# A hybrid retention and attention layer on one core: the first retention head's queries and keys move behind the attention branch's projection, four more gates become attention fillers whose results are put aside in device memory, and inputs and first weights alternate in one queue

## The chip, the cores and the metric

The kernel runs on one core of one Trainium2 chip. The metric is device time in microseconds, the median over runs of the whole program. The kernel before took 1144.44 us (three runs: 1139.92, 1144.44 and 1145.31). Of one execution there is a profile, taken by the hardware profiler. In the text, PE is TensorE's matrix multiplication and PEld its loading of weights, DVE is VectorE, ACT is ScalarE, POOL is GpSimd and SP is SyncE.

## The reference, cut to what matters

One layer over 512 tokens with a model width of 1024. Two branches read the same normalised input through one combined projection; each is projected back, gated, and their sum goes through an output projection. An MLP and a gated embedding follow.

```python
h = rms_norm(x, norm_mix)
rq, rk, rv, rg, cq, ckv, krope, gr, gm = jnp.split(h @ w_in, offsets, axis=-1)

rq = rope(rq, pos); rk = rope(rk, pos) * 256 ** -0.5      # 4 heads, 256 wide
ro = retention(rq, rk, rv)                                # chunks of 128 tokens, decay
a_ret = (rms_norm(ro, ret_norm) * silu(rg)) @ w_br        # w_br: 2048 x 1024

q = (rms_norm(cq, q_lat_norm) @ w_uq); kv = rms_norm(ckv, kv_lat_norm) @ w_ukv
mo = causal_block_attention(...)                          # 8 heads
a_mla = mo @ w_bm

mixed = sigmoid(gr) * a_ret + sigmoid(gm) * a_mla
x = x + mixed @ w_o
x = x + square(relu(rms_norm(x, norm_mlp) @ w_up)) @ w_down
x = x + sigmoid(rms_norm(x, norm_ple) @ w_ple_gate) * (p_l @ w_ple)
```

## The kernel before, in words

Activations lie with channels on the 128 partitions and the 512 tokens along the row, so a vector of 1024 channels is eight tiles of 128x512. Every product is made of three matmuls (`mm3`): an operand is split into a high and a low part, and low x high, high x low and high x high are accumulated in a PSUM bank. A projection of one tile of outputs from eight tiles of inputs is therefore 24 matmuls of 128x512. The high part of a tile is an ACT copy, the low part a DVE subtraction that follows it (`split`, L308 and L309 in the profile; for weights `load_chunk`, L265 and L267).

**The program order.** The kernel is a list of steps, written out by hand. A step may have a weight chunk. `run_steps` loads the chunk of the step after the current one (AHEAD = 1) before it emits the current step, so an engine's queue holds, in this order, the split of the next weights and then the work of this step. Each engine runs its queue strictly in order. Where nothing binds an instruction to its place (`keep_in_program_order`), the program's builder may put it ahead of steps before it, so the queues as built are shown with the change. Weight halves lie in NW = 3 rotating buffers each for high and low parts, the raw weights in NRAW = 6; taking a buffer waits for its former user. The raw weights come in by DMAs on SP's queue.

**Chunks that are sums.** The projections rv and rg (retention's values and gates) and the down projection are made by a seven-product scheme on 2x2 blocks. Its operands are sums and differences of blocks: of weights, by one DMA and a second one that accumulates on top of it, which POOL issues (`("sw", …)`, prepared PREP = 3 ahead); of activations, by `x_operand(p)`, p = 1 to 7, from the normalised input tiles `xr` (f32) and `xn` (their split, made by `norm_x`).

**Stages on PE**, in order of time: the first projection `a1` (tile pA), for which the input tiles `x` are multiplied by a gain and split (`xg`, L311) while the sum of squares is still to come; latents; eight attention heads, where softmax leaves gaps that **fillers** use; `branch_m` (tile bm, the attention branch's projection); then for two pairs of heads rv, and for each of the four heads rq, rk, rg, scores, and the former head's `branch_r` (tile br); then the gates gr and the last `branch_r`; out_proj (tile wo); the MLP (up, dn) and the gated embedding.

**Fillers** are half projections (12 matmuls each) from `xg`, the input that isn't yet divided by its root mean square; the result is multiplied by `rbc` (that factor, broadcast). Before there are 26 of them: the gates gm of the attention branch (8 x 2 halves, each result put in device memory by `aside`, a DMA that POOL issues), rq and rk of retention head 0 (4 x 2 halves), and the gate gr0 (2 halves). EARLY = 1 is the number of gr gates among the fillers.

**Tiles.** A pool T has 45 rotating tiles of 128x512 (NDYN), a pool K 16 (NKEEP). xg, and later xn, x_operands and much else lie in them.

**The tail before the output projection.** `reload(n)` brings back ret (the sum of the first three heads' branch_r, tile re) and the gated attention branch (tile ze), 16 loads on SP's queue. Then come the gates gr1 and gr2, and four steps of `branch_r(3)`, each of which makes two tiles of 24 matmuls together, with the gates gr3 to gr7 and `mix` between them. `ret_factor(3)` splits the last head's output (tiles og to rog) after gr1. `mix(n)` multiplies ret by the gate, adds the attention branch and splits the result (tile mix), which out_proj reads.

**The start.** ACT's queue issues the eight loads of x and the gains before its first arithmetic; SP's queue issues the weights wr_a. A DMA is issued only when the eighth DMA before it, of all queues, has landed.

Of the kernel before, what the change touches and what calls it, by code (L numbers as in the profile page):

```python
# [37 lines left out]
P = 128  # L38
S = 512
# [14 lines left out]

NDYN, NKEEP, NW, NRAW, NDRAW, AHEAD, PREP, EARLY, PAD = 45, 16, 3, 6, 4, 1, 3, 1, 104
GROUPS = DFF // 1024
# [14 lines left out]
def chunk_specs():  # L71
# [32 lines left out]
    for h in range(RH):  # L104
        for key, o in (("rq", O_RQ), ("rk", O_RK)):
            for n in range(2):
                if h:
                    add((key, h, n), "w_in", full, _rng(o + h * RQK + n * P, P))
                else:
                    for k in range(2):  # L110
                        add((key, h, n, k), "w_in", _rng(k * S, S), _rng(o + h * RQK + n * P, P))
        for k in range(4):
            add(("br", h, k), "w_br", _rng(h * RV, RV), _rng(2 * k * P, 2 * P))
# [38 lines left out]
def trunk_layer(ctx: ExitStack, tc: tile.TileContext, xT, pT, pos, gains, const, decay, wstream, outT):  # L152
# [207 lines left out]
    for k in range(8):  # L360
        xs.append(T(f"x{k}"))
        tc.keep_in_program_order(nc.scalar.dma_start(xs[k], xT[:, k]))
        if k == 0:
            tc.keep_in_program_order(nc.scalar.dma_start(gn, gains))
        if k < 6:
            prepare(("a1", k))
    tc.keep_in_program_order(nc.sync.dma_start(cst, const))
    tc.keep_in_program_order(nc.sync.dma_start(posi, pos.partition_broadcast(P)))
# [333 lines left out]
    def x_operand(p):  # L702
# [9 lines left out]
        for c in range(2):  # L712
            t = T(f"sy{c}") if p == 5 else V["sx"][c]
            for kk in range(2):
# [7 lines left out]
                else:  # L722
                    TT(o, xr[4 + k][:, lo_], o, op=ALU.subtract)

            new = T if p == 7 else K
            hl = split(t, None, hi=new(f"s{p}{c}h", F32R), lo=new(f"s{p}{c}l", F32R))
            XS[p].extend(cut(hl, kk * 256, 256) for kk in range(2))
# [36 lines left out]

    def ret_qk(w, h, key, n, half=None):
        d = R[h]
        if half is None:
            ps = proj(B(f"{key}{h}{n}"), xn, w)
        else:
            if half == 0:  # L770
                d["half"] = B(f"{key}{h}{n}")
            ps = proj(d["half"], xg, w, k0=4 * half, k1=4 * half + 4)
            if half == 0:
                return
        a, b = T(f"{key}a{h}{n}"), T(f"{key}b{h}{n}")
        TT(a, ps, V["cr"] if n == 0 else V["sr"], op=ALU.mult)
        TT(b, ps, V["sr"] if n == 0 else V["cr"], op=ALU.mult)
        if n == 0:
            d[key] = (a, b)
        else:  # L780
            a0, b0 = d[key]
            TT(a0, a0, a, op=ALU.subtract)
            TT(b0, b0, b, op=ALU.add)
            if half is not None:
                TT(a0, a0, V["rbc"], op=ALU.mult)
                TT(b0, b0, V["rbc"], op=ALU.mult)
            d[key] = (split(a0, f"{key}x{h}"), split(b0, f"{key}y{h}"))
# [64 lines left out]
    def ret_factor(h):  # L852
        d, r = R[h], R[h]["r"]
        bc = bcast(B(f"pbo{h}"), lambda b: r[:, b:b + 1])
        for m in range(4):
            TT(d["og"][m], d["og"][m], bc, op=ALU.mult)
            new = K if m < 2 else T
            d["rog"][m] = split(d["og"][m], None, hi=new(f"rog{h}{m}h", F32R), lo=new(f"rog{h}{m}l", F32R))

# [14 lines left out]
    def reload(n):  # L874
        for l, nm in ((ret, "re"), (zm, "ze")):
            t = T(f"{nm}{n}")
            nc.sync.dma_start(t, l[n])
            l[n] = t

    def gate_r(w, n, half=None):  # L880
        if half is None:
            ps = proj(B(f"gr{n}"), xn, w)
        else:
# [3 lines left out]
            if half == 0:  # L887
                return
        sgr[n] = T(f"gr{n}")
        if half is None:  # L890
            ACT(sgr[n], ps, AF.Sigmoid)
        else:
            TT(sgr[n], ps, V["rbc"], op=ALU.mult)

# [193 lines left out]
    fillers = [(("gm", n, half), gate_m, n, half) for n in range(8) for half in range(2)]  # L1088
    fillers += [((key, 0, n, half), ret_qk, 0, key, n, half) for key in ("rq", "rk") for n in range(2) for half in range(2)]

    fillers += [(("gr", n, half), gate_r, n, half) for n in range(EARLY) for half in range(2)]
# [37 lines left out]
    for h in range(MH):  # L1129
        p, more = h // 2, h + 2 < MH  # L1130
        step(None, scores, h)
        if h % 2 == 0:
# [12 lines left out]
            if h == 0:  # L1145
                fill(1)
            step(None, transposes, h)
            if h == 2:
                step(None, rotary_out, 1)
            if h:  # L1150
                fill(1)
        else:
# [25 lines left out]
    for n in range(8):  # L1178
        step(("bm", n), branch_m, n)
        if n < 2:  # L1180
            step(None, norm_x, 2 + n)
        elif n == 2:
            step(None, x_operand, 7)
        elif n < 7:
            step(None, norm_x, n + 1)
    for p in (1, 2, 6, 5, 4, 3):
        step(None, x_operand, p)
    for h in range(RH):
        for key in ("rq", "rk"):
            for n in range(2 if h else 0):  # L1190
                step((key, h, n), ret_qk, h, key, n)
                if (key, n) == ("rq", 0):
                    step(None, ret_factor, h - 1)
# [19 lines left out]
    for n in range(8):  # L1213
        step(None, reload, n)
    for n in range(EARLY, EARLY + 2):
        step(("gr", n), gate_r, n)
        if n == EARLY:
            step(None, ret_factor, RH - 1)
    for k in range(4):
        step(("br", RH - 1, k), branch_r, RH - 1, k)  # L1220
        step(None, mix, 2 * k)
        for n in (EARLY + 2 * k + 2, EARLY + 2 * k + 3):
            if n < 8:
                step(("gr", n), gate_r, n)
        step(None, mix, 2 * k + 1)
# [107 lines left out]
```

## Time and profile before

| | us |
|---|---|
| median of three runs | 1144.44 |
| the profiled execution | 1137.74 |
| its span (first to last instruction) | 1136.0 |
| outside the span | 1.74 |

| engine | busy us | share |
|---|---|---|
| PE | 1103.0 | 97% |
| DVE | 736.8 | 65% |
| ACT | 535.7 | 47% |
| POOL | 83.0 | 7% |

The granted clock of TensorE had a mean of 0.998 over the span. Stages on PE: first projection from 11.4 us, attention with its fillers from 56 to 242, branch_m from 242 to 285.7, retention to 636, gates and the last branch_r to 698, output projection to 742, MLP to 1084.

How to read it: busy times of the engines overlap, so they do not add up to the span. A matmul that is shown with 0.39 us starts 0.227 us after the one before it, since matmuls are pipelined, and a window counts those that only reach into it. "idle before" is the time in which an engine's queue stood, and the name behind it is the instruction for which it stood.

### The profile page before, as it was taken

The numbers are of one execution on the slowest core, as the hardware profiler recorded it, in microseconds if no ns is written. First come the engines' busy times: TensorE is split into PE (matmuls) and PEld (weight loads), VectorE is DVE, ScalarE is ACT, GpSimd is POOL, SyncE is SP. The second block draws the span as 40 slices with busy tenths as digits, with TensorE's granted clock in tenths as the row PEclk, the third lists the DMA queues.
The fourth block names the chain that finished last, engine by engine and source line by source line (L and its number), as shares of the span: only waits on it lengthen the run. The fifth ranks groups of instructions, "written<-read, shape, count | busy, mean of one in ns | idle before, by whom it ended". The sixth has DMA issues, their size and how long they took to land.

```text
span 1136.0 us, 14670 instructions
## 1 busy us (share of the span) xinstructions
PE 1103.0 (97%) x5540; PEld 935.0 (82%) x5540; DVE 736.8 (65%) x1205; ACT 535.7 (47%) x762; POOL 83.0 (7%) x108
## 2 busy tenths in 40 slices
PE   5999989999799999999999999999999999999998
PEld 4887878888589899889989888888888888888877
DVE  5787686766667746636764756546566566668775
ACT  5555656454456345445544423434444443445542
POOL 0000000001210110121011000010100100101000
PEclk9999999999999999999999999999999999999999
DMA  7223131258893463698367623584755755737501
GB/s 227 75 87 132 61 93 48 77 174 238 213 240 113 132 200 112 152 242 206 117 172 161 253 91 123 189 263 147 155 160 176 178 159 161 183 130 211 145 35 74
DMA packets 58104, 173.35 MB, mean 153 GB/s; under 512 B 7089, under 2 KB 8497, under 8 KB 57777
## 3 DMA queue, kind: packets, MB, share of 16 engines
q1 hardware_dynamic: 43296, 126.25, 32.6%
q0 software_dynamic: 13440, 44.05, 20.4%
q10 hardware_dynamic: 1296, 2.12, 0.5%
q8 instruction: 43, 0.70, 0.2%
q14 instruction: 29, 0.23, 0.1%
HBM read 155.61 MB, written 14.68 MB: 150 GB/s over the span
## 4 chain that ended last, share of the span: by engine, by line
PE 89%; DMA 4%; DVE 3%; ACT 2%; issue 1%; SPq 0%; POOL 0%; ACTq 0%; POOLq 0%
PE up L172 15%; PE dn L172 13%; PE br L172 8%; PE rg L172 7%; PE rv L172 6%; PE pg L172 4%; PE rq L172 4%; PE rk L172 4%; PE wo L172 3%; PE gr L172 3%; PE gm L172 3%; PE ro L172 3%; PE sc L172 2%; PE pA L172 2%; PE pcq L172 1%; PE bm L172 1%
## 5 line engine op out<-in xcount | busy, mean ns | idle before, releaser
L172 PE MATMUL dn<-wh_dn,cl 128*128 128x512 f32 x224 | 87.2, 389 | 0.0
L172 PE MATMUL dn<-wh_dn,ch 128*128 128x512 f32 x224 | 87.2, 389 | 0.0
L172 PE MATMUL dn<-wl_dn,ch 128*128 128x512 f32 x224 | 87.1, 389 | 0.0
L265 ACT ACTIVATE wh_dn<-wr_dn 128x1024 fp32r<-128x1024 f32 x32 | 34.0, 1063 | 75.4 <-PE up L172 54.3
L265 ACT ACTIVATE wh_up<-wr_up 128x1024 fp32r<-128x1024 f32 x32 | 34.0, 1061 | 57.7 <-PE up L172 29.0
L267 DVE TENSOR_TENSOR wl_dn<-wr_dn,wh_dn 128x1024 fp32r<-128x1024 f32 x32 | 39.1, 1220 | 26.8 <-ACT wh_dn L265 26.8
L267 DVE TENSOR_TENSOR wl_up<-wr_up,wh_up 128x1024 fp32r<-128x1024 f32 x32 | 39.1, 1223 | 18.6 <-ACT wh_up L265 18.6
L172 PEld LDWEIGHTS dn<-wh_dn,ch 128*128 128x128 f32 x224 | 42.0, 188 | 8.8
L172 PEld LDWEIGHTS dn<-wh_dn,cl 128*128 128x128 f32 x224 | 42.0, 188 | 8.8
L172 PEld LDWEIGHTS dn<-wl_dn,ch 128*128 128x128 f32 x224 | 42.0, 188 | 8.6
L959 DVE SCALAR_TENSOR_TENSOR f<-up,bcx 128x512 f32<-128x512 f32 x32 | 20.6, 686 | 43.8 <-PE up L172 43.8
L267 DVE TENSOR_TENSOR wl_rg<-wr_rg,wh_rg 128x1024 fp32r<-128x1024 f32 x20 | 24.3, 1223 | 34.7 <-ACT wh_rg L265 34.6
L227 POOL DMA_DIRECT2D dr_dn<-wstream x24 | 21.4, 893 | 331.6 <-DVE rx L330 137.5
L265 ACT ACTIVATE wh_dn<-dr_dn 128x1024 fp32r<-128x1024 f32 x24 | 25.5, 1061 | 42.6 <-PE up L172 28.8
L267 DVE TENSOR_TENSOR wl_dn<-dr_dn,wh_dn 128x1024 fp32r<-128x1024 f32 x24 | 29.3, 1222 | 23.0 <-ACT wh_dn L265 23.0
L265 ACT ACTIVATE wh_rg<-wr_rg 128x1024 fp32r<-128x1024 f32 x28 | 29.4, 1055 | 26.8 <-DMA wr_rg<-wstream 14.3
L265 ACT ACTIVATE wh_rv<-wr_rv 128x1024 fp32r<-128x1024 f32 x28 | 29.6, 1057 | 19.2 <-PE rv L172 11.9
L1017 DVE TENSOR_TENSOR d<-d,dn 128x1024 f32<-128x1024 f32 x24 | 29.3, 1219 | 6.4 <-PE dn L172 6.4
L267 DVE TENSOR_TENSOR wl_rv<-wr_rv,wh_rv 128x1024 fp32r<-128x1024 f32 x20 | 24.5, 1224 | 12.2 <-ACT wh_rv L265 12.2
L866 ACT ACTIVATE rt<-br 128x512 f32<-128x512 f32 x24 | 14.4, 598 | 36.1 <-PE br L172 31.2
L267 DVE TENSOR_TENSOR wl_br<-wr_br,wh_br 128x1024 fp32r<-128x1024 f32 x16 | 19.5, 1220 | 16.6 <-ACT wh_br L265 16.6
L639 ACT ACTIVATE p<-p,ng,hr 128x128 f32<-128x128 f32 (+3 forms) x32 | 20.6, 645 | 15.8 <-DVE ng L637 15.8
(1911 smaller groups left out, 3607.5 us busy)
## 6 DMA issues: line engine op xcount, KB each, us to landing
wr_up<-wstream SPq DMA_DIRECT2D x32, 512.0 KB, 4.0
wr_dn<-wstream SPq DMA_DIRECT2D x32, 512.0 KB, 3.4
dr_dn<-wstream POOLq DMA_DIRECT2D x24, 512.0 KB, 7.7
wr_rv<-wstream SPq DMA_DIRECT2D x20, 512.0 KB, 3.8
wr_rg<-wstream SPq DMA_DIRECT2D x20, 512.0 KB, 4.6
wr_rv<-wstream POOLq DMA_DIRECT2D x16, 512.0 KB, 6.7
wr_rg<-wstream POOLq DMA_DIRECT2D x16, 512.0 KB, 6.8
wr_br<-wstream SPq DMA_DIRECT2D x16, 512.0 KB, 3.6
```

The source lines that it names most:

```text
L172: return tc.keep_in_program_order(nc.tensor.matmul(*a, **k))
L227: nc.gpsimd.dma_start(raw, chunk(("w", blk, kb, fb, c)), accum_op=ALU.add)
L265: ACT(hi, raw, AF.Copy, scale=sign)
L267: TT(lo, raw, hi.bitcast(F32), op=ALU.subtract)
L639: ACT(cols[b], cols[b], AF.Exp, bias=ng[:, b:b + 1], scale=d["rq"][:, b], accum_out=sums[:, b:b + 1])
L866: ACT(t, ps, AF.Copy)
L959: STT(u[:, i], ps[:, i], 0.0, V["bcx2"], op0=ALU.max, op1=ALU.mult)
L1017: TT(to, to, dps[p], op=ALU.add if sign > 0 else ALU.subtract)
```

## The change

Five edits.

1. **EARLY from 1 to 5, and head 0's rq and rk out of the fillers.** The gates gr1 to gr4 become fillers beside gr0: 10 halves in all, each finished gate is multiplied by rbc and put aside in device memory (gr0 too), and `reload` brings the five back (tiles ge; 21 loads in place of 16). rq and rk of head 0, 8 halves before, become four full projections from xn behind branch_m and ahead of the first rv step, as those of the other heads. There are 26 halves among the fillers before and after.
2. **The loads of x** go on SP's queue, one behind each of the first weight chunks. The gains stay on ACT's queue.
3. **Where tiles lie.** All splits of x_operands are in K (before, those of p = 7 were in T); all splits of rog are in T (before, half of them in K). All `norm_x` steps now stand between the branch_m steps, and all x_operands behind them (before, x_operand 7 stood after the third).
4. **At head 2** the filler comes before rotary_out.
5. **In the tail** the gates gr5, gr6 and gr7 all stand ahead of the last branch_r; before, gr1 and gr2 did and gr3 to gr7 stood between its steps.

```diff
-NDYN, NKEEP, NW, NRAW, NDRAW, AHEAD, PREP, EARLY, PAD = 45, 16, 3, 6, 4, 1, 3, 1, 104
+NDYN, NKEEP, NW, NRAW, NDRAW, AHEAD, PREP, EARLY, PAD = 45, 16, 3, 6, 4, 1, 3, 5, 104
...
     for k in range(8):
         xs.append(T(f"x{k}"))
-        tc.keep_in_program_order(nc.scalar.dma_start(xs[k], xT[:, k]))
-        if k == 0:
-            tc.keep_in_program_order(nc.scalar.dma_start(gn, gains))
         if k < 6:
             prepare(("a1", k))
+        tc.keep_in_program_order(nc.sync.dma_start(xs[k], xT[:, k]))
+    nc.scalar.dma_start(gn, gains)
...
-            new = T if p == 7 else K
-            hl = split(t, None, hi=new(f"s{p}{c}h", F32R), lo=new(f"s{p}{c}l", F32R))
+            hl = split(t, None, hi=K(f"s{p}{c}h", F32R), lo=K(f"s{p}{c}l", F32R))
...
-            if half is not None:
-                TT(a0, a0, V["rbc"], op=ALU.mult)
-                TT(b0, b0, V["rbc"], op=ALU.mult)
...
-            new = K if m < 2 else T
-            d["rog"][m] = split(d["og"][m], None, hi=new(f"rog{h}{m}h", F32R), lo=new(f"rog{h}{m}l", F32R))
+            d["rog"][m] = split(d["og"][m], f"rog{h}{m}")
...
     def reload(n):
-        for l, nm in ((ret, "re"), (zm, "ze")):
+        for l, nm in ((ret, "re"), (zm, "ze"), (sgr, "ge")):
+            if l is sgr and n >= EARLY:
+                continue
...
-            TT(sgr[n], ps, V["rbc"], op=ALU.mult)
+            TT(t, ps, V["rbc"], op=ALU.mult)
+            sgr[n] = aside(f"gr{n}", t)
...
-    fillers += [((key, 0, n, half), ret_qk, 0, key, n, half) for key in ("rq", "rk") for n in range(2) for half in range(2)]
-
     fillers += [(("gr", n, half), gate_r, n, half) for n in range(EARLY) for half in range(2)]
...
             step(None, transposes, h)
+            if h:
+                fill(1)
             if h == 2:
                 step(None, rotary_out, 1)
-            if h:
-                fill(1)
...
         step(("bm", n), branch_m, n)
-        if n < 2:
+        if n < 6:
             step(None, norm_x, 2 + n)
-        elif n == 2:
-            step(None, x_operand, 7)
-        elif n < 7:
-            step(None, norm_x, n + 1)
-    for p in (1, 2, 6, 5, 4, 3):
+    for p in (1, 7, 2, 6, 5, 4, 3):
         step(None, x_operand, p)
     for h in range(RH):
         for key in ("rq", "rk"):
-            for n in range(2 if h else 0):
+            for n in range(2):
                 step((key, h, n), ret_qk, h, key, n)
-                if (key, n) == ("rq", 0):
+                if h and (key, n) == ("rq", 0):
                     step(None, ret_factor, h - 1)
...
-    for n in range(EARLY, EARLY + 2):
+    for n in range(EARLY, 8):
         step(("gr", n), gate_r, n)
         if n == EARLY:
             step(None, ret_factor, RH - 1)
     for k in range(4):
         step(("br", RH - 1, k), branch_r, RH - 1, k)
         step(None, mix, 2 * k)
-        for n in (EARLY + 2 * k + 2, EARLY + 2 * k + 3):
-            if n < 8:
-                step(("gr", n), gate_r, n)
         step(None, mix, 2 * k + 1)
```

The lists below show what stands in an engine's queue, in program order; an instruction is written as its line, operation, output <- inputs and shape, and a number at the end of a name only tells buffers apart. Line numbers after the change are a few lower for the same code.

At the start of the program, on ACT before the change (x are the input tiles, wr_a the raw first weights, wh_a their high parts, xg0h the high part of the first input times its gain):

```order
L362 DMA x_113<-xT 128x512
L362 DMA x_115<-xT 128x512
L265 ACT_TABLE_LOAD
L265 ACTIVATE wh_a_0_119<-wr_a_0_91 128x384
L311 ACTIVATE xg0h<-x_88,gn 128x512
L265 ACTIVATE wh_a_1_127<-wr_a_1_95 128x384
L311 ACTIVATE xg1h<-x_93,gn 128x512
```

The same place on ACT after the change:

```order
L361 DMA gn<-gains 128x50
L261 ACT_TABLE_LOAD
L261 ACTIVATE wh_a_0_119<-wr_a_0_89 128x384
L261 ACTIVATE wh_a_1_127<-wr_a_1_93 128x384
L261 ACTIVATE wh_a_2_135<-wr_a_2_97 128x384
L307 ACTIVATE xg0h<-x_88,gn 128x512
L307 ACTIVATE xg1h<-x_92,gn 128x512
```

The loads of x have left the queue, the load of the gains is alone ahead of the table load, and the splits of the second and third weight chunk have moved ahead of xg0h.

Behind branch_m, on DVE before the change (s, sx, sy are x_operands and their sums, gb the gated attention branch, wl_rv the low part of the fifth rv chunk):

```order
L721 TENSOR_TENSOR sy_3023<-xr_2728,xr_2959 128x256
L723 TENSOR_TENSOR sx_2773<-xr_2911,sx_2773 128x256
L723 TENSOR_TENSOR sx_2773<-xr_2959,sx_2773 128x256
L309 TENSOR_TENSOR s50l<-sy_3016,s50h 128x512
L685 TENSOR_TENSOR gb_2973<-gb_2973,bm_2975 128x512
L309 TENSOR_TENSOR s51l<-sy_3023,s51h 128x512
L267 TENSOR_TENSOR wl_rv_3106<-wr_rv_3067,wh_rv_3105 128x1024
```

The same place on DVE after the change, where rqa and rqb are rq's two products with the rotary factors and wl_rk_0 the low part of the weights for the first half of rk:

```order
L305 TENSOR_TENSOR s60l<-sx_2963,s60h 128x512
L762 TENSOR_TENSOR rqa_3046<-rq_3021,trc 128x512
L305 TENSOR_TENSOR s61l<-sx_2964,s61h 128x512
L718 TENSOR_TENSOR sx_2963<-xr_2750,sx_2963 128x256
L305 TENSOR_TENSOR s50l<-sy_2989,s50h 128x512
L718 TENSOR_TENSOR sx_2963<-xr_2794,sx_2963 128x256
L305 TENSOR_TENSOR s51l<-sy_2996,s51h 128x512
L718 TENSOR_TENSOR sx_2964<-xr_2838,sx_2964 128x256
L305 TENSOR_TENSOR s30l<-sx_2963,s30h 128x512
L718 TENSOR_TENSOR sx_2964<-xr_2882,sx_2964 128x256
L763 TENSOR_TENSOR rqb_3047<-rq_3021,trs 128x512
L263 TENSOR_TENSOR wl_rk_0_3053<-wr_rk_0_3050,wh_rk_0_3052 128x1024
```

rq's work and rk's weights are new there; wl_rk_0 stands behind the x_operands, and on PE rq follows the last bm where rv did.

In the tail, on ACT before the change (wr_gr and wh_gr are a gate's raw weights and their high part, the line L891 is the sigmoid of a gate, rog30h to rog33h the last head's splits):

```order
L265 ACTIVATE wh_br_0_6284<-wr_br_0_6282 128x1024
L265 ACTIVATE wh_gr_6317<-wr_gr_6315 128x1024
L308 ACTIVATE rog30h<-og_6008 128x512
L308 ACTIVATE rog31h<-og_6025 128x512
L265 ACTIVATE wh_gr_6358<-wr_gr_6356 128x1024
L891 ACTIVATE gr_6255<-gr_6230 128x512
L308 ACTIVATE rog32h<-og_6043 128x512
L308 ACTIVATE rog33h<-og_6061 128x512
```

The same place on ACT after the change (ge are the reloaded gates, whose sigmoid is L883):

```order
L261 ACTIVATE wh_br_0_6465<-wr_br_0_6463 128x1024
L883 ACTIVATE ge_6334<-ge_6334 128x512
L883 ACTIVATE ge_6340<-ge_6340 128x512
L883 ACTIVATE ge_6346<-ge_6346 128x512
L261 ACTIVATE wh_br_1_6498<-wr_br_1_6496 128x1024
L883 ACTIVATE ge_6352<-ge_6352 128x512
L883 ACTIVATE ge_6358<-ge_6358 128x512
L261 ACTIVATE wh_br_2_6546<-wr_br_2_6544 128x1024
L875 ACTIVATE gr_6403<-gr_6378 128x512
L304 ACTIVATE rog30h<-og_6146 128x512
L304 ACTIVATE rog31h<-og_6163 128x512
```

All weights are now those of br, the five sigmoids of reloaded gates stand among them, and rog30h stands behind the third of them.

More of the change, by code (lines that the diff above doesn't have):

```diff
@@ L106, in chunk_specs @@
             for n in range(2):
-                if h:
[L108 to L111, printed above, removed]
+                add((key, h, n), "w_in", full, _rng(o + h * RQK + n * P, P))
         for k in range(4):
@@ L763, in ret_v, with ret_qk @@
                     R[2 * q + blk % 10 - 1].setdefault("v", [None] * 4)[2 * (blk // 10 - 1) + i] = split(t, f"rv{q}{blk}{i}")
-    def ret_qk(w, h, key, n, half=None):
+    def ret_qk(w, h, key, n):
         d = R[h]
[L767 to L774, printed above, removed]
+        ps = proj(B(f"{key}{h}{n}"), xn, w)
         a, b = T(f"{key}a{h}{n}"), T(f"{key}b{h}{n}")
@@ L888, in gate_r @@
                 return
-        sgr[n] = T(f"gr{n}")
+        t = T(f"gr{n}")
         if half is None:
-            ACT(sgr[n], ps, AF.Sigmoid)
-        else:
-            TT(sgr[n], ps, V["rbc"], op=ALU.mult)
+            ACT(t, ps, AF.Sigmoid)
+            sgr[n] = t
+        else:
+            TT(t, ps, V["rbc"], op=ALU.mult)
+            sgr[n] = aside(f"gr{n}", t)
     def mix(n):
@@ L1147, in trunk_layer @@
             step(None, transposes, h)
+            if h:
+                fill(1)
             if h == 2:
                 step(None, rotary_out, 1)
-            if h:
-                fill(1)
         else:
```

## Prediction

> **What bounds the kernel now.** I read the page first, for the span and the chain that ended last; then what PE waits for; then windows of 10 us at those waits; then the timelines of the engines that PE waits for.
>
> ```profile
> span 1136.0 us, 14670 instructions
> PE 89%; DMA 4%; DVE 3%; ACT 2%; issue 1%; SPq 0%; POOL 0%; ACTq 0%; POOLq 0%
> ```
>
> The bound is PE's own work. The change leaves the matmuls as they are in number and shape (head 0's rq and rk are 8 halves of 12, later 4 of 24), so it can act only on the stalls. These are PE's waits; the columns behind the colon are the sum in us, how many, and the longest.
>
> ```profile
> PE pA L172 <- ACT xg0h L311: 11.4, 1, 11.4
> PE rv L172 <- DVE wl_rv L267: 6.8, 2, 5.3
> PE mo L172 <- DVE zm L674: 2.9, 1, 2.9
> PE rv L172 <- ACT wh_rv L265: 1.4, 1, 1.4
> PE br L172 <- ACT rog32h L308: 0.8, 1, 0.8
> PE br L172 <- DVE rog32l L309: 0.4, 1, 0.4
> PE wo L172 <- DVE mix7l L309: 0.2, 1, 0.2
> ```
>
> That is the start, the first rv step, one place in attention and the tail. What a stall costs is more than the wait, since the clock may fall and waits inside a chunk are short. The windows count it: matmuls in PE's first bracket, granted clock after the busy times.
>
> ```profile
> 280.00:290.00 10.00, 10.00 (x46) 8.29 (x45) 8.38 (x14) 4.96 (x7) 2.00 (x3) 1.00 0.78 214
> 290.00:300.00 10.00, 7.06 (x31) 5.23 (x29) 6.20 (x12) 3.67 (x5) 3.21 (x4) 1.00 1.04 262
> 300.00:310.00 10.00, 4.72 (x14) 3.53 (x13) 7.13 (x10) 6.54 (x11) 1.09 (x2) 0.83 0.59 154
> 310.00:320.00 10.00, 9.99 (x44) 7.86 (x44) 6.30 (x8) 6.37 (x8) 1.22 (x2) 1.00 0.93 214
> 640.00:650.00 10.00, 9.05 (x41) 6.95 (x39) 6.45 (x9) 5.01 (x8) 0.00 (x0) 1.00 1.04 395
> 650.00:660.00 10.00, 9.74 (x43) 8.07 (x44) 6.60 (x10) 2.06 (x4) 0.00 (x0) 1.00 0.48 181
> 700.00:710.00 10.00, 9.78 (x43) 7.76 (x43) 5.59 (x7) 3.51 (x5) 0.00 (x0) 1.00 0.56 184
> ```
>
> A full window has 46, so one missing matmul is 10/46 = 0.217 us. The rv step lacks 15 + 32 + 2 = 49, which is **10.7 us**, of which 6.8 + 1.4 = 8.2 are waits and 2.5 the lower clock (0.83) and small gaps. The tail lacks 5 + 3 + 3 = 11, which is **2.4 us**.
>
> **The change part by part. The start: -3.5.** The engines' timelines (start, duration) and the landing times of the weights:
>
> ```profile
> 1.66 7.14 ACTq L362 DMA_DIRECT2D x<-xT  x7
> 8.82 1.28 ACT L265 ACT_TABLE_LOAD   x1 [8.82 <-DMA x<-xT]
> 10.12 0.52 ACT L265 ACTIVATE wh_a<-wr_a 128x384 fp32r<-128x384 f32 x1
> 10.55 0.71 ACT L311 ACTIVATE xg0h<-x,gn 128x512 fp32r<-128x512 f32 x1
> 11.38 0.77 PE L172 MATMUL pA<-xg0h,wl_a 128*128 128x512 f32 x1 [11.38 <-ACT xg0h L311]
> 1.18 0.90 SPq L247 DMA_DIRECT2D wr_a<-wstream  x2
> wr_a<-wstream SPq DMA_DIRECT2D x1, 192.0 KB, 5.2
> DMA to landing us min/median/max: 2.5/4.3/5.8
> ```
>
> ACT issues x until 8.8 us, then loads its table, splits one weight chunk and makes xg0h; PE starts 0.83 us after xg0h does. Without the x loads ACT loads its table at about 1.2. In the new order three weight splits stand ahead of xg0h, so it waits for wr_a 2. SP's issues are 0.45 us each (0.90 for the second and third), the first at 0.73; wr_a 2 is now the fifth, at 0.73 + 4 x 0.45 = 2.5. It lands after 2.5 us (the fastest of all) to 5.2 (its own time before), so at 5.0 to 7.7; I take 6.6, nearer to its own. Then 0.5 for the split and 0.83: PE starts at 7.9, 3.5 earlier (bounds -2.2 to -4.9). [...]
>
> **The first rv step: -8.6.** PE runs from bm straight into rv, whose weights and x_operands are made meanwhile on DVE:
>
> ```profile
> 296.06 1.22 DVE L267 TENSOR_TENSOR wl_rv<-wr_rv,wh_rv 128x1024 fp32r<-128x1024 f32 x1
> 297.19 0.68 DVE L309 TENSOR_TENSOR xn7l<-xr,xn7h 128x512 fp32r<-128x512 f32 x1
> 297.79 0.69 DVE L309 TENSOR_TENSOR s61l<-sx,s61h 128x512 fp32r<-128x512 f32 x1
> 298.39 1.42 DVE L721 TENSOR_TENSOR sy<-xr,xr 128x256 f32<-128x256 f32 x4
> 681.61 5.44 PE br L172 x24
> DMA to landing us min/median/max: 3.4/5.5/10.0
> ```
>
> A DVE operation of 512 columns takes 0.60 from start to start, one of 256 about 0.34, a weight's low part 1.13 (1.22 to its end). The row of br is 24 matmuls, 5.44 us; the last is for rv's raw weights with those that POOL adds. Now four projections, 4 x 5.44 = 21.8 us, lie between bm and rv. With R as rv's start, product 6's sum is issued when product 7's split is done, at R + 2.3, and lands at R + 7.8 (5.5, the median) or R + 12.3 (10.0). Its split is due 2.3 us ahead of its matmuls at R + 16.3, so at R + 14.0: 1.7 us or more to spare, and the 10.7 us go.
>
> What is late next is rk. Call T0 the end of the last bm. wh_rk_0 takes the buffer that bm's last weights hold until T0 (three buffers), and the x_operand s70h and the next stand behind it on ACT; their low parts, and behind these wl_rk_0, on DVE. The first low part starts at T0 + 1.06 + 0.62 + 0.07 = T0 + 1.75 (a weight's split, a 512-wide one, the hand-over). Ahead of wl_rk_0 are 11 operations of 512 and 9 of 256: 11 x 0.60 + 9 x 0.34 = 9.7. wl_rk_0 then ends at T0 + 1.75 + 9.7 + 1.22 = T0 + 12.6, and some operations wait for an ACT result made just before, which I put at 0.4: T0 + 13.0. rk is due at T0 + 2 x 5.44 = T0 + 10.9. The new stall is **2.1 us** (bounds 0.9, if ACT runs ahead, to 4), so -10.7 + 2.1 = -8.6.
>
> **The tail: +2.1.** ACT, DVE and SP in the tail before:
>
> ```profile
> 647.28 1.06 ACT L265 ACTIVATE wh_gr<-wr_gr 128x1024 fp32r<-128x1024 f32 x1 [3.57 <-DMA re<-ret6d]
> 648.25 0.58 ACT L891 ACTIVATE gr<-gr 128x512 f32<-128x512 f32 x1
> 648.72 0.62 ACT L308 ACTIVATE rog32h<-og 128x512 fp32r<-128x512 f32 x1
> 649.52 0.69 DVE L309 TENSOR_TENSOR rog32l<-og,rog32h 128x512 fp32r<-128x512 f32 x1
> 636.10 0.33 SPq L877 DMA_DIRECT2D re<-ret0d  x1
> 645.20 0.32 SPq L877 DMA_DIRECT2D ze<-am7d  x1
> DMA to landing us min/median/max: 3.7/5.1/5.7
> ```
>
> After, three gates run from 636 to G = 636 + 3 x 5.44 = 652.3. wh_br_2 takes the buffer of the third gate's weights, free at G, and behind it on ACT stand a sigmoid and the splits of rog: 1.06 + 0.58 + 0.62, so rog30h is done at G + 2.3; its low part stands behind wl_br_2 on DVE and is done at G + 3.1. Stall 3.0. Later no gate's matmuls lie between the br steps: DVE has 8 mix steps of four 512-wide operations and four weight parts, 32 x 0.60 + 4 x 1.13 = 23.7, with about 1 us of waits for ACT 24.7, from the first finished br tile (2.7 after br's start U). mix7's low part ends 0.7 behind that, at U + 28.1, and is due at U + 4 x 5.44 + 7 x 3 x 0.227 = U + 26.6: stall 1.5 ahead of wo. Together 4.5 in place of 2.4.
>
> For that, the reloads must be in time. Their 16 issues went from 636.10 to 645.20, 0.61 each; the 15th of 21, the fifth gate, is issued 8.5 us after the first, lands 3.7 to 5.7 later, at 648.3 to 650.3, ahead of G by 2.0 or more. The sum of reload, DVE and POOL work for the gates is hidden: POOL is busy for 7% of the span, and the five multiplications in the fillers take no more than rk's and rq's did.
>
> **Attention: 0.** PE waits 2.9 us for zm, which stood behind rotary_out's first operation on DVE:
>
> ```profile
> 148.89 0.75 DVE L552 SCALAR_TENSOR_TENSOR o<-pqa,gn,tmc 128x512 f32<-128x512 f32 x1 [1.53 <-PE sc L172]
> 155.85 0.69 DVE L674 TENSOR_TENSOR zm<-gm,rbc 128x512 f32<-128x512 f32 x1
> 156.45 0.28 DVE L633 CUSTOM_DVE_ANT_0 p<-sc,kf 128x128 f32<-128x128 f32 x1
> ```
>
> Now zm goes first, but rotary's tile takes zm's buffer and waits for its transfer, so rotary starts at about 149.6 in place of 148.9, and the softmax chain behind it (p) where it did: PE's wait moves on to that chain. Bounds: -2.9, all won, and +1.
>
> The tiles that change pools (s7 out of T, rog into it: four tiles each) cost nothing while T's 45 suffice; if not, that is the last rival. **Sum:** -3.5 - 8.6 + 2.1 = -10.0. The profiled execution would take 1137.74 (span and 1.74 around it) - 10.0 = 1127.7. The median of the runs is 1144.44, 6.7 above it; on that footing **1134.4 us**.
>
> **Rivals.** (a) The rv weights are late anyway. POOL now has five asides ahead of the first accumulating load, where one stood, and the slowest sum took 10.0 to land. Against: 21.8 us of cover. Then the 8.6 go: 1134.4 + 8.6 = **1143.0**. This is also the case in which the change doesn't do what it says. (b) Attention's stall is won: the softmax chain is shorter than I take it. 1134.4 - 2.9 = **1131.5**. (c) DVE's backlog ahead of rk is 4 us or more and the clock falls with it, as it did in rv: 4.0 + 2.5 in place of 2.1, **1138.8**. [...] For: the walk above counts 9.7 us of DVE work. (d) Slower: the tail's reloads wait for T tiles. 16 xn, 21 reloads, 4 og and 4 z make 45, all there are. If one more is held, the loads start when the last gate frees xn, at G; the sigmoid of the fifth reloaded gate, ahead of wh_br_2 and rog30h on ACT, then has its data at G + 8.5 + 3.7 to 5.7, and br starts 3.1 after that, at G + 15 to 17. In place of 3.0 that is 13 more, with the lower clock 2.5: 1134.4 + 15.5, about **1150.5**. It decides from a delay of the reloads by over 2.0 us on, and each further us costs one.
>
> **How the numbers follow.** Forecast 0.48, (a) 0.18, (b) 0.12, (c) 0.13, (d) 0.09. A measurement of this kernel can tell about 0.5% (5.7 us) from no change, so "faster" is below 1138.7. Faster: 0.46 of the forecast, all of (b), half of (c): 0.65. Slower: (d)'s longer half and more, and little else: 0.08. Same: the rest, 0.27. The range takes in (b) with the start's better bound (1131.5 - 1.4) and some 2 us of spread between medians, 1128, and (a) with the start's worse bound, 1144; outside are (d) and the edges of (a) and (b), some 0.2.
>
> **What would show it.** In the changed kernel: PE's first matmul at 7 to 9 us, behind xg0h; no wait of rv on wl_rv above 1 us, and 300 to 320 full at clock 1.00; a wait of rk on wl_rk_0 of about 2 us; br waiting some 3 us for rog30h or rog30l and wo some 1.5 for mix7l. Wrong are: a first matmul past 10 (x itself comes late on SP), rv waits beyond 3 us (a), rk's beyond 4 (c), or reloads that land after G (d).

## The result, and the profile after

The changed kernel takes 1135.93 us (median of four runs, 1134.84 to 1136.53); beside it the kernel before took 1143.99 (1139.92 to 1145.31). The ratio is 0.9934, 95% interval [0.9908, 0.9961]: 4.5 to 10.5 us faster. Later pairs of the same two kernels on one chip gave 0.9957 [0.9941, 0.9973] and 0.9951 [0.9931, 0.9970], so 0.5% is nearer to the truth than 0.7%. The forecast was 1134.4.

The two profiled executions differ far less: spans of 1136.0 and 1134.0, only 2.0 us. So the result has two halves: what the change does to one execution, and why the kernel before is mostly slower than its profiled execution. First the page of the changed kernel, its span and its chain:

```profile
span 1134.0 us, 14681 instructions
PE 89%; DVE 5%; DMA 3%; issue 2%; ACT 1%; SPq 0%; DVEq 0%; ACTq 0%
```

DVE has taken over a part of what transfers had in the chain. PE's waits in the changed kernel (sum in us, how many, the longest):

```profile
PE pA L168 <- ACT xg0h L307: 8.9, 1, 8.9
PE rk L168 <- DVE wl_rk L263: 6.2, 1, 6.2
PE br L168 <- ACT rog30h L304: 2.1, 1, 2.1
PE pt3a L168 <- DVE p L637: 1.3, 1, 1.3
...
PE up L168 <- DVE xr L897: 0.8, 1, 0.8
PE sqr L168 <- DVE mx L628: 0.8, 1, 0.8
...
PE wo L168 <- DVE mix7l L305: 0.6, 1, 0.6
PE wo L168 <- ACT mix7h L304: 0.4, 1, 0.4
PE br L168 <- DVE rog30l L305: 0.4, 1, 0.4
```

All 8.2 us of rv's waits are gone, and rk waits 6.2 in their place. The windows of the changed kernel at the stalls (matmuls in PE's first bracket, granted clock behind the busy times):

```profile
290.00:300.00 10.00, 3.81 (x15) 2.84 (x14) 10.00 (x21) 5.34 (x8) 0.53 (x1) 0.80 0.18 56
300.00:310.00 10.00, 10.00 (x39) 8.09 (x39) 7.59 (x10) 2.29 (x3) 0.51 (x1) 0.86 0.46 159
310.00:320.00 10.00, 10.00 (x46) 8.28 (x45) 7.15 (x9) 5.48 (x8) 2.98 (x4) 1.00 0.99 191
...
660.00:670.00 10.00, 7.85 (x35) 6.19 (x33) 2.84 (x4) 5.32 (x9) 0.00 (x0) 1.00 1.05 403
670.00:680.00 10.00, 9.65 (x35) 7.58 (x35) 6.66 (x11) 3.96 (x7) 0.00 (x0) 0.83 0.31 118
680.00:690.00 10.00, 10.00 (x46) 8.29 (x45) 9.79 (x15) 4.02 (x5) 0.00 (x0) 1.00 0.31 105
690.00:700.00 10.00, 9.36 (x41) 7.17 (x39) 10.00 (x16) 3.60 (x5) 0.00 (x0) 1.00 0.16 50
700.00:710.00 10.00, 9.69 (x42) 7.99 (x43) 5.80 (x8) 4.50 (x6) 0.00 (x0) 1.00 0.71 230
```

Counted as in the forecast, against 46 in a full window: behind branch_m 31 + 7 = 38 are missing, 8.3 us, in place of 10.7 before; in the tail 11 + 11 + 5 + 4 = 31, 6.7 us, in place of 2.4. The first matmul comes 2.5 earlier. In attention mo's 2.9 and pt3a's 0.5 (a row of the same view before, which the forecast didn't need) became 0.8 and 1.3: 1.3 less. The sum is -2.5 - 1.3 - 2.4 + 4.3 = -1.9, and the spans differ by 2.0. The new wait of up, 0.8, is not balanced in this sum, so it is good to about 1 us.

Why does rk wait 6.2 and not 2.1? The timelines of DVE, ACT and SP in the changed kernel, in this order (start, duration, in brackets the idle time before and what ended it):

```profile
283.55 0.68 DVE L305 TENSOR_TENSOR s70l<-sx,s70h 128x512 fp32r<-128x512 f32 x1
287.62 0.69 DVE L680 TENSOR_TENSOR gb<-gb,bm 128x512 f32<-128x512 f32 x1 [3.38 <-ACT gb L679]
...
297.48 1.21 DVE L263 TENSOR_TENSOR wl_rk<-wr_rk,wh_rk 128x1024 fp32r<-128x1024 f32 x1
...
286.96 0.63 ACT L679 ACTIVATE gb<-gb 128x512 f32<-128x512 f32 x1 [3.61 <-DMA gb<-zm6d]
...
269.14 0.37 SPq L692 DMA_DIRECT2D xr<-xT  x1
274.40 4.59 SPq L233 DMA_DIRECT2D wr_rv<-wstream  x2
279.40 0.33 SPq L677 DMA_DIRECT2D gb<-zm6d  x1
```

Two loads of rv weights stand in SP's queue ahead of the load of branch_m's gate gb6. They wait for buffers of raw weights, which DVE's wl_rq frees (SP's waits for it there: 8.7 us in two). The first was issued only at 274.40, 5 us behind the load before it; the gate's load went at 279.40 and landed at 286.9. ACT's sigmoid of it, DVE's product of gb, and behind that the x_operands and wl_rk_0 waited in turn. DVE stood for 3.4 us in the middle of the queue that the forecast had counted as work without a gap.

### The profile page after: what moved, and what is told of

Its sections match the earlier page's. It is cut to its first block, busy times and chain, and to the rows that moved or that the text cites. A ratio compares the mean times of both kernels' runs of the same rounds, so it can differ in the third digit from the quotient of the medians.

```text
span 1134.0 us, 14681 instructions
## 1 busy us (share of the span) xinstructions
PE 1104.4 (97%) x5540; PEld 936.1 (83%) x5540; DVE 735.7 (65%) x1205; ACT 537.5 (47%) x762; POOL 85.5 (8%) x113
## 4 chain that ended last, share of the span: by engine, by line
PE 89%; DVE 5%; DMA 3%; issue 2%; ACT 1%; SPq 0%; DVEq 0%; ACTq 0%
PE up L168 15%; PE dn L168 13%; PE rg L168 7%; PE rv L168 7%; PE br L168 6%; PE rk L168 4%; PE pg L168 4%; PE wo L168 3%; PE bm L168 3%; PE rq L168 3%; PE gm L168 3%; PE ro L168 3%; PE gr L168 2%; PE sc L168 2%; PE pA L168 2%
```

## The experiments

Each was timed in five rounds beside the kernel before; "ratio" is against that kernel on the same chip. In the diffs a minus is the changed kernel's line, where nothing else is said.

**The kernel before, again** (e1_before), without an edit.

> The kernel before, unchanged, to see another of its executions. Its profiled execution took 1137.74 us, 6.25 below its median of 1143.99, and the one of the changed kernel 1135.76, at its own median. Theory: the kernel before varies in its stalls, above all where rv waits for sums of weights that are still on the way, so that this profile shows some 3 to 6 us more stall than the first (8.2 us of waits in rv, 11.4 at the start, 1.4 in the tail), and the time is 1142 to 1145. Rival: the stalls are those of the first profile within 1 us each and the time is 1137 to 1139 here too, so that the offset belongs to the place where it was measured, and the gain of the change is about 2 us on one chip.

Its twelve runs lie between 1138.62 and 1146.77 (median 1143.26, ratio 1.0009 [0.9991, 1.0026]), and its profiled execution took 1144.87, with a span of 1143.1. Two things are in it that the first profile hadn't. Waits, windows and ACT's timeline of this execution:

```profile
PE ro L172 <- ACT ath L308: 2.7, 2, 1.4
...
150.00:160.00 10.00, 7.11 (x43) 5.63 (x42) 8.89 (x22) 3.98 (x10) 0.54 (x1) 0.86 0.28 82
550.00:560.00 10.00, 10.00 (x64) 9.61 (x62) 4.89 (x8) 5.38 (x10) 0.00 (x0) 0.84 0.31 105
...
353.59 1.06 ACT L265 ACTIVATE wh_rg<-wr_rg 128x1024 fp32r<-128x1024 f32 x1 [2.48 <-DMA wr_rg<-wstream]
354.56 0.40 ACT L308 ACTIVATE ath<-s 128x256 fp32r<-128x256 f32 x1
```

The first windows of the kernel before, for the same stretches:

```profile
150.00:160.00 10.00, 7.11 (x57) 6.21 (x50) 8.53 (x23) 4.57 (x11) 0.54 (x1) 1.00 0.30 87
550.00:560.00 10.00, 10.00 (x83) 9.82 (x82) 7.67 (x20) 4.81 (x8) 0.00 (x0) 1.00 0.21 63
```

The wait of mo for zm, 2.9 us in both, cost the clock in one execution (0.86, 43 matmuls in place of 57) and not in the other. And in heads 0 and 2 ro waited (1.3 and 1.4 us) for the last split ath, which stands on ACT behind a weight split that waits for its transfer; the clock fell after the second of these waits (0.84). rv's stall was no larger (its two waits sum to 8.5, with wh_rv's 1.4 gone). Both profiles hold the same matmuls in the same order, so the start times of each can be compared: the second execution falls behind by 1.4 us at mo, by 1.7 and 3.0 at the two waits of ro, by 0.2 in rv and by about 0.6 in the first 6 us of PE's work. That is nearly all of the 7.1 by which the spans differ. So the theory was right that the kernel before varies, and, for these two executions, wrong that it varies in rv.

**The changed kernel, again** (e2_after), without an edit.

> The changed kernel, unchanged. Theory: its stalls repeat (start 8.9 us, rk 6.2, the first br of the tail 2.5 in sum, wo 1.0) within about 0.5 us each, since they come from the order of the queues and not from one late transfer; 1135 to 1137 us. Rival: the wait of rk for wl_rk (6.2) comes from one transfer that landed late by chance (the load of gb6 took 7.5 us), and is 2 to 4 us in another execution, 1131 to 1133.

1136.00 (1134.94 to 1138.62), ratio 0.9957 [0.9941, 0.9973]; waits of 8.7 at the start, 6.0 at rk, 2.1 + 0.4 at br, 0.6 + 0.4 at wo. The stalls repeat, as they would if the queues' order makes them and not one late transfer. What doesn't repeat is the clock behind br's waits, 1.00 here and 0.83 in the changed kernel's first profile:

```profile
670.00:680.00 10.00, 8.52 (x36) 6.81 (x37) 8.13 (x12) 5.28 (x10) 0.00 (x0) 1.00 0.44 167
```

**The last head's rog in K** (e3_rogk).

```diff
-            d["rog"][m] = split(d["og"][m], f"rog{h}{m}")
+            new = K if h == RH - 1 else T
+            d["rog"][m] = split(d["og"][m], None, hi=new(f"rog{h}{m}h", F32R), lo=new(f"rog{h}{m}l", F32R))
```

> The changed kernel with the splits of the last head's rog in the pool K, all eight. Theory: in the tail the splits wait for buffers of T that the last gate frees, and not for their turn behind wh_br_2; with buffers of their own they are made while the gates run, the first br waits for nothing (2.5 us of waits gone), and TensorE's clock stays at 1.00 there, where the window 670 to 680 shows 0.83 (about 1.7 us): 3 to 4.5 us faster than the changed kernel, wo's wait may grow by up to 0.5. Rival, as the forecast has it: the order on ACT (wh_br_2, a sigmoid, rog30h) makes the wait whatever the buffers; no change within 1 us.

1131.47 (1131.24 to 1131.99), ratio 0.9916 [0.9901, 0.9932], 4.5 us below e2_after on the same chip. The window that had 0.83 is full, and no wait of br is left:

```profile
670.00:680.00 10.00, 10.00 (x46) 8.28 (x45) 8.85 (x13) 3.95 (x7) 0.00 (x0) 1.00 0.56 202
```

So the splits waited for buffers of T. On ACT rog30h now starts at 658.79 and wh_br_2 at 668.66: with buffers of its own the split also stands earlier in the queue. wh_br_2 ahead of rog30h, which the forecast took for the cause, seems to be only where the builder put an instruction that had to wait for a buffer anyway; the edit changed nothing but the buffers.

**The x_operands spread over rq and rk** (e4_spread).

```diff
-    for p in (1, 7, 2, 6, 5, 4, 3):
-        step(None, x_operand, p)
+    late = [(1, 7, 2), (6,), (5, 4), (3,)]
...
                 step((key, h, n), ret_qk, h, key, n)
+                for p in late.pop(0) if late else ():
+                    step(None, x_operand, p)
```

> The changed kernel with the x_operands taken from ahead of head 0's rq and rk and put one to three behind each of these four steps. Theory: the wait of rk for wl_rk (6.2 us) is DVE's queue of x_operands ahead of it, held up 3.4 us more by the sigmoid of gb6; wl_rk_0 is then made ahead of them, the wait goes, the clock stays at 1.00, and the time falls by 6 to 8 us. Rival: the work is only put off, and rv then waits for its x_operands (s70 is needed 5.4 us behind rv's start) or for product 6's sums: 0 to 3 us faster.

1135.04 (1133.60 to 1138.66), ratio 0.9951 [0.9934, 0.9968]: the rival. rk no longer waits, and rv does:

```profile
PE rv L168 <- DVE wl_rv L265: 5.5, 1, 5.5
...
290.00:300.00 10.00, 10.00 (x46) 8.27 (x45) 10.00 (x20) 4.20 (x7) 0.54 (x1) 1.00 0.44 149
300.00:310.00 10.00, 6.95 (x31) 5.43 (x29) 10.00 (x20) 6.14 (x9) 0.91 (x1) 1.00 0.44 95
310.00:320.00 10.00, 7.58 (x22) 6.07 (x23) 6.08 (x8) 3.05 (x5) 2.61 (x3) 0.66 0.63 127
```

DVE is busy for 20 us on end in both windows. The order of its work was changed, its sum and the idle time ahead of it weren't.

**The pools alone, on the kernel before** (e5_before_pools; the minus is the kernel before).

```diff
-            new = T if p == 7 else K
+            new = K
...
-            new = K if m < 2 else T
+            new = T
```

> The kernel before with one part of the change alone: the splits of x_operand 7 lie in K and those of rog in T. On ACT this puts the last of the four splits ath of heads 0 and 2 ahead of the weight split wh_rg, which waits for a transfer; before, it stood behind it. In the second profile of the kernel before, ro waited for ath there, 1.35 and 1.49 us, and the clock fell behind the second (0.84); in the first profile neither was seen. Theory: these waits make a part of the spread of the kernel before (1138 to 1147); they are gone here in every execution, the spread narrows to some 4 us and the median falls by 1 to 3, less 1 to 2 that the last br loses with rog in T. The stalls of rv stay (8 to 9 us with the clock). Rival: the spread comes from rv's stalls alone; median and spread as before, within 1 us, or 1 to 2 slower for the tail.

1140.89 (1135.95 to 1141.77), ratio 0.9982 [0.9965, 1.0000]. No wait of ro above 0.3 us is in its profile, the upper end of the runs came down from 1147 to 1142, and the median by about 1, with br now waiting 2.1 + 0.3 for rog where it waited 0.8 + 0.4. mo's wait with the fallen clock is still there (0.86 in 150 to 160). Set against e1_before's profile matmul by matmul, rv's stall is about 2.5 us shorter, which wasn't expected, the two places of ro give 1.9 and 3.5, and the last branch_r costs 2.6: in the tail the pools alone, with the old order of the gates, make br wait as it does in the changed kernel.

**The loads of x back on ACT's queue** (e6_x_act), the second part of the change undone.

```diff
+        tc.keep_in_program_order(nc.scalar.dma_start(xs[k], xT[:, k]))
+        if k == 0:
+            tc.keep_in_program_order(nc.scalar.dma_start(gn, gains))
         if k < 6:
             prepare(("a1", k))
-        tc.keep_in_program_order(nc.sync.dma_start(xs[k], xT[:, k]))
-    nc.scalar.dma_start(gn, gains)
```

> The changed kernel with the loads of x back on ACT's queue. Theory: the first matmul is at 10.9 to 11.4 us again in place of 8.7 to 8.9, and all that follows comes 2.2 to 2.6 us later: 1138 to 1139. Rival: the later start is made up, since what PE waits for next (the DVE's queue ahead of rk) doesn't come later with it: below 1 us.

1137.11 (1136.38 to 1138.35), ratio 0.9958 [0.9943, 0.9973]. The first matmul is at 11.0 in place of 8.6 to 8.9, 2.1 to 2.4 later:

```profile
PE pA L168 <- ACT xg0h L307: 11.0, 1, 11.0
```

The profiled span is 1135.0 in place of 1133.9 (e11_after), 1.1 longer, so about half of what the start gives reaches the end. Against e11_after, matmul by matmul, the 2.4 us are 2.0 after PE's first 6 us, 1.5 behind rk and 1.1 at the end: the rest is made up in several places, and rk's wait (5.5 here, 5.4 there) doesn't account for it. The medians of this one and of the changed kernel lie too close for their intervals; only the traces, one execution each, tell them apart.

**The loads of branch_m's gates two steps earlier** (e7_gb).

```diff
-        t = T(f"gb{n}")
-        nc.sync.dma_start(t, zm[n])
+        t = gb[n]
...
+    step(None, load_gb, 0)
+    step(None, load_gb, 1)
     for n in range(8):
+        if n < 6:
+            step(None, load_gb, n + 2)
         step(("bm", n), branch_m, n)
```

> The changed kernel with branch_m's loads of its gates (gb) issued two steps earlier, ahead of the rv weights that stood before gb6 in SP's queue. Theory: DVE's 3.4 us without work ahead of the gate's product (it waited for the load of gb6, which came behind two rv weights) go, and rk's wait falls from 6.0 to 2.6 or less, about what the forecast had (2.1); with a shorter wait the clock behind it stays near 1.00 (0.76 to 0.86 before): 3.5 to 5 us faster than the changed kernel. Rival: DVE's 9.7 us of x_operands alone make the wait, or the loads of x7 and xn come later behind the gates; less than 1.5 us faster.

1129.23 (1128.91 to 1130.35), ratio 0.9887 [0.9856, 0.9918]: 6.6 to 6.8 us below the changed kernel's 1135.79 and 1136.00, which were measured on other chips. The wait of rk, the windows behind it and the products of gb6 and gb7 on DVE (in the changed kernel at 287.62 and 289.00):

```profile
PE rk L168 <- DVE wl_rk L263: 1.4, 1, 1.4
...
290.00:300.00 10.00, 8.57 (x38) 6.77 (x37) 10.00 (x17) 3.74 (x6) 0.00 (x0) 1.00 0.41 115
300.00:310.00 10.00, 10.00 (x46) 8.29 (x45) 6.98 (x10) 3.38 (x4) 1.76 (x2) 1.00 0.71 196
...
277.67 0.69 DVE L685 TENSOR_TENSOR gb<-gb,bm 128x512 f32<-128x512 f32 x1 [0.24 <-PE bm L168]
283.36 0.68 DVE L685 TENSOR_TENSOR gb<-gb,bm 128x512 f32<-128x512 f32 x1
```

gb6's product comes 10 us earlier, right behind its own matmuls (bm), and gb7's 5.6 earlier without idle time ahead. 8 matmuls are missing in place of 38, 6.5 us. The gain is larger than the 3.4 us of idle time: rk's wait is 4.8 us shorter, and the clock no longer falls (1.00 in both windows, where the changed kernel had 0.80 and 0.86).

**Three edits together** (e8_best): e3_rogk, e7_gb, and the x_operands put near their use. The first four of the list stand behind head 0's rq and rk, the others behind rv's steps.

```diff
+    late = [(1, 7), (), (), (2,), (6,), (5,), (4, 3)]
...
                 step(("sw", ("rv", h // 2), p, c), ret_v, h // 2, p, c)
+            for p_ in late.pop(0) if late else ():
+                step(None, x_operand, p_)
```

> The changed kernel with three edits: rog of the last head in K (as e3_rogk, 4.5 us faster), gb loaded two steps earlier (as e7_gb), and the x_operands put where they are needed: 1 and 7 behind rq's first step, 2, 6, 5, 4 and 3 behind steps of rk and rv. Theory: the stall between bm and rv was DVE's queue, in e4_spread only moved from rk (6.2) to rv (5.5) because DVE still had the same work and the same idle 3.4 us ahead; with the idle time gone and some 5 us of x_operands moved behind rv's start neither rk nor rv waits over 1 us, and the clock stays at 1.00: 1122 to 1126. Rival: rv still waits 2 us or more, for products' sums or late x_operands: 1127 to 1131.

1123.34 (1123.18 to 1124.18), ratio 0.9835 [0.9804, 0.9866]. Neither rk nor rv nor br waits:

```profile
290.00:300.00 10.00, 10.00 (x46) 8.29 (x45) 10.00 (x18) 4.95 (x7) 0.00 (x0) 1.00 0.54 161
300.00:310.00 10.00, 10.00 (x46) 8.29 (x45) 9.79 (x16) 4.94 (x7) 2.83 (x4) 1.00 0.69 136
310.00:320.00 10.00, 10.00 (x45) 8.28 (x45) 6.74 (x11) 6.88 (x10) 1.52 (x2) 1.00 1.00 236
```

DVE is nearly as full as in e4_spread, but its first x_operand starts at 289.02 in place of 290.89, fewer x_operands stand ahead of rv, and PE doesn't stand.

**The order at head 2 as before** (e9_swap), the fourth part undone.

```diff
-            if h:
-                fill(1)
             if h == 2:
                 step(None, rotary_out, 1)
+            if h:
+                fill(1)
```

> The changed kernel with the order at head 2 as before: rotary_out ahead of the filler. Theory: the exchange gives about half of the 2.9 us that mo waited for zm, and pays the rest back in waits of the softmax chain (in the changed kernel 0.83 at sqr and 1.46 at pt3a, in place of 2.94 at mo and 0.71 at pt3a): this kernel is 1.2 to 1.6 us slower than the changed one at that place, though what follows (rk, behind DVE's queue) may take part of it back. Rival, the forecast's: the wait only moves, no difference (within 0.5 us) at that place.

1137.32 (1135.13 to 1140.23), ratio 0.9959 [0.9943, 0.9974]. At the place itself the theory holds: mo waits 2.9 and pt3a 0.5 again, and what follows comes 1.3 us later than in the changed kernel (rk here waits 7.0). At the end of the profiled executions nothing of it is left: the span is 1133.9 here as in e11_after, and the 0.8 to 1.2 us that PE waits for up in the profiles of the changed kernel are missing here. The runs spread over 5 us, those of the changed kernel beside them over 4, so the medians' 1.5 us is inside the noise.

**All but the move and the tail, on the kernel before** (e10_no_move): x on SP, both pools, norm_x ahead of the x_operands, the order at head 2. Head 0's rq and rk stay fillers, EARLY stays 1, and the tail keeps its old order. Of the change's diff the first and the fifth part are left out, among them these two pieces:

```diff
-    fillers += [((key, 0, n, half), ret_qk, 0, key, n, half) for key in ("rq", "rk") for n in range(2) for half in range(2)]
...
-    for n in range(EARLY, EARLY + 2):
+    for n in range(EARLY, 8):
```

> The kernel before with all parts of the change but the first and the tail's: x on SP's queue, x_operand 7 in K and rog in T, norm_x ahead of all x_operands, the exchange at head 2; head 0's rq and rk are still fillers, gr0 the only gate among them, the tail in its old order. Theory: what moves rq and rk behind branch_m gives little by itself as it was built: here rv waits for 5 to 8 us with the clock falling behind it, where the changed kernel has rk's 6.0; the time is 1136 to 1139, within 2 of the changed kernel. Rival, the forecast's: the move is the largest part, 8.6 us of the gain; then this kernel is at 1141 or more (the changed one and 5 us or more).

1135.84 (1134.12 to 1136.13), ratio 0.9939 [0.9915, 0.9963], the same as the changed kernel beside it (1135.79). rv waits here, for the same late gate: DVE stood 3.39 us for gb.

```profile
PE rv L172 <- DVE wl_rv L267: 8.0, 2, 7.5
...
280.00:290.00 10.00, 8.46 (x38) 6.67 (x36) 5.71 (x12) 3.52 (x6) 2.34 (x3) 1.00 0.82 222
290.00:300.00 10.00, 4.09 (x10) 3.29 (x11) 9.62 (x19) 6.70 (x11) 2.00 (x3) 0.53 0.63 134
300.00:310.00 10.00, 9.41 (x40) 7.44 (x39) 6.25 (x7) 4.79 (x6) 1.75 (x2) 0.95 0.80 187
310.00:320.00 10.00, 9.99 (x45) 7.87 (x44) 6.15 (x8) 6.37 (x8) 0.86 (x1) 1.00 0.91 218
...
640.00:650.00 10.00, 7.50 (x33) 5.63 (x32) 6.15 (x9) 4.15 (x7) 0.00 (x0) 1.00 1.04 407
```

Counted as before, rv lacks 8 + 36 + 6 + 1 = 51 matmuls, 11.1 us, where the changed kernel's rk lacks 8.3; the tail lacks 13, 2.8 us, where the changed kernel's lacks 6.7. So the move gives 2.8 us behind branch_m, and the new tail takes 3.9.

**The changed kernel a third time** (e11_after).

> The changed kernel again, to stand beside the three others on one chip, and beside e6_x_act: 1135 to 1137, start 8.3 to 9.3, rk 5.5 to 6.3. If it is within 0.5 us of e6_x_act's 1137.1, the start's 2.2 us are made up later; if it is 1135 or less they are not.

1135.79 (1134.85 to 1138.95), ratio 0.9951 [0.9931, 0.9970]; start 8.6, rk 5.4. It is 1.3 below e6_x_act's median, which comes from another chip: the start is neither lost nor whole.

**The tail interleaved again** (e12_tail), on e8_best: gr7 goes behind the first step of the last branch_r.

```diff
-    for n in range(EARLY, 8):
+    for n in range(EARLY, EARLY + 2):
         step(("gr", n), gate_r, n)
...
         step(None, mix, 2 * k)
+        for n in (EARLY + 2 * k + 2, EARLY + 2 * k + 3):
+            if n < 8:
+                step(("gr", n), gate_r, n)
```

> The kernel of e8_best with the tail's old interleaving: gr7 stands behind the first step of the last branch_r in place of ahead of it. Theory, by the forecast's second term of the tail: DVE's mix steps are short of the time of one gate's matmuls; with one gate (5.4 us) between the br steps the waits of wo for mix7 (0.60 and 0.85 in e8_best) go, 1.0 to 1.5 us, 1121.5 to 1122.5. Rival: mix waits for reloaded tiles or buffers instead, no gain or 1 us slower.

1122.62 (1121.50 to 1123.03), ratio 0.9826 [0.9800, 0.9853], against e8_best's 1123.34 on another chip. wo's waits are one of 1.0 in place of 1.0 in sum, the wait of up (0.8) is gone, and two of 0.4 and 0.5 at rv are new. That this edit gives anything is not shown.

## Why the prediction was right or wrong

**The time** was right, 1134.4 against 1135.93, and the range held it; the way to it was right only in part, and that the number comes so near is luck. The forecast had 10.0 us for the change in one execution, where the two profiles show 2.0; what fills the gap in the medians (see the footing below) was not in the forecast.

**The start, -3.5**: right in mechanism, too large. The first matmul came 2.5 us earlier in the profile (at 8.3 to 9.6 in all profiles with x on SP's queue, at 10.9 to 11.4 in those without). wr_a 2 landed just ahead of 7.68, where ACT's timeline has its split, at the late bound of 7.7 and not at 6.6; the time that it took before was the one to take:

```profile
7.68 0.52 ACT L261 ACTIVATE wh_a<-wr_a 128x384 fp32r<-128x384 f32 x1 [1.76 <-DMA wr_a<-wstream]
8.11 0.71 ACT L307 ACTIVATE xg0h<-x,gn 128x512 fp32r<-128x512 f32 x1
```

Of this, e6_x_act shows 1.1 at the end of its profile, and 1.3 between medians from two chips.

**rv, -8.6**: wrong, and this is the step that failed. That rv's stall would go was right; "the new stall is 2.1 us" was not. The walk of DVE's queue counted the work ahead of wl_rk_0 and took the sigmoid of gb6 as ready. It was behind a load that two rv weights held up in SP's queue, and the 3.4 us of idle time that came of it, with the fallen clock (0.80 and 0.86), made 8.3 us of 2.1. The last bm ended at 281.5 and wl_rk_0 at 298.7, 17.2 behind it where the forecast had 13.0: 4.2 more, of which DVE's idle times ahead of gb6 and gb7 are 3.4 and 0.7. e7_gb takes that away and leaves a wait of 1.4, inside the bounds (0.9 to 4): the walk itself was sound. What happened is rival (c), with a mechanism that the forecast didn't name. e10_no_move shows how little was left: without the move and without the new tail the kernel is as fast.

**The tail, +2.1**: right in sign, too small, +4.3 in the profile. Both stalls came where they were forecast, br 2.5 (3.0) and wo 1.0 (1.5). Two things were wrong in it: the cause of the first was T's buffers and not ACT's order (e3_rogk; e5_before_pools has br's waits with the old order of the gates), and the clock fell behind it in the profiled execution (0.83), which the forecast had only in its rivals (c) and (d). That the tiles that change pools "cost nothing while T's 45 suffice" was the wrong step; rog's own move into T was what they didn't suffice for. (d) didn't come, and its price was added up wrongly: 1134.4 + 15.5 is 1149.9 and not 1150.5. The data of the fifth reloaded gate were there 2.3 us ahead of the last gate's end (667.5; its last matmul starts at 667.25), against 2.0 in the forecast, as ACT's timeline shows; wh_br_2 waited for PE alone:

```profile
665.24 0.63 ACT L883 ACTIVATE ge<-ge 128x512 f32<-128x512 f32 x1 [1.35 <-DMA ge<-gr4d]
667.68 1.06 ACT L261 ACTIVATE wh_br<-wr_br 128x1024 fp32r<-128x1024 f32 x1 [1.81 <-PE gr L168]
```

**Attention, 0**: wrong at the place, -1.3 (e9_swap). PE's wait was cut into 0.8 and 1.3, and not moved whole. At the end of the span e9_swap's profile shows nothing of it.

**The footing.** The forecast carried -10.0 from the profiled execution over to the median. In the profiled executions the change is worth 2.0. The rest lies in what the first profile didn't show: two waits in the kernel before that are long in some executions, or take the clock along in some. The pools end the waits of ro (e5_before_pools: upper end 1142 for 1147), and the exchange at head 2 breaks up mo's 2.9 us. Neither was in the sum. On the profile's footing the forecast was 1127.7, and the profiled execution of the changed kernel took 1135.76, 8 us more; the median hid that. How the 8 us of the medians, 5 to 6 in the later pairs, divide among these parts is not settled to better than 1 us each: the intervals are as wide as the parts.

## What to carry to other kernels

A queue walk must take in what each instruction on it waits for, down to the queue that issues its load: one late load in the middle of DVE's queue undid most of the largest term. One profile of a kernel whose runs spread over 8 us is one sample: look in a second for waits that the first lacks, and for instructions that stand behind a transfer (here ath behind wh_rg) and were in time by luck. Moving matmuls into a gap helped here only as far as the engine that prepares their operands had time (rk waited 6.2 us for DVE); spread that engine's work to where it is needed, and move the loads ahead, as e8_best does (1123.34, 1.65% below the kernel before).

## What the hardware showed that wasn't expected

The clock fell after shorter waits than the forecast reckoned with, and not each time. mo's wait of 2.9 us left it at 1.00 in one execution of the kernel before and at 0.86 (over 10 us) in another; br's 2.1 and 0.4 left it at 0.83 in one of the changed kernel and at 1.00 in the second; rk's 1.4 alone left it at 1.00 (e7_gb), and ro's 1.4 in e1_before was followed by 0.84. The same wait at the same place was thus followed by a lower clock in one execution (0.86) and not in another (1.00); what decides it, no run here shows. The price was 1.4 us behind mo's wait, by the start times of the same matmuls in the two executions, and up to 2.5 in rv of the kernel before (0.83), small gaps included.
